# Layer 1's recurrent mixer in another order: four heads' scans at once, a gate pair between the heads' matrices, its convolution and its squares in PSUM

## The chip, the cores and the metric

The kernel runs on one core of a Trainium2 chip. The metric is the device time of one execution in microseconds (us), as the median of several runs. The engines are called PE (TensorE: matmuls, and PEld for its weight loads), DVE (VectorE), ACT (ScalarE), POOL (GpSimd) and SP (SyncE, which issues the loads here).

## What is computed

One sequence of 256 tokens of width 1024 goes through two residual layers and then a second block. Layer 0 has a convolution and an attention mixer, layer 1 the recurrent mixer `mixer_c`; each is followed by a squared-ReLU MLP of width 4096. The change touches layer 1's mixer and the end of each MLP.

```python
def rg_lru(x, w_r, b_r, w_i, b_i, lam):
    """x: (B, S, W). h_t = a_t h_{t-1} + sqrt(1-a_t^2) (i_t x_t)."""
    b, s, w = x.shape
    xb = x.reshape(b, s, LRU_HEADS, LRU_BLOCK)          # 8 heads of 128
    r = jax.nn.sigmoid(jnp.einsum("bshi,hij->bshj", xb, w_r) + b_r).reshape(b, s, w)
    i = jax.nn.sigmoid(jnp.einsum("bshi,hij->bshj", xb, w_i) + b_i).reshape(b, s, w)
    log_a = -LRU_C * r.astype(jnp.float32) * jax.nn.softplus(-lam.astype(jnp.float32))
    a = jnp.exp(log_a)
    mult = jnp.sqrt(-jnp.expm1(2.0 * log_a))
    bx = mult * (i * x).astype(jnp.float32)
    ...
    _, hseq = lax.associative_scan(combine, (a, bx), axis=1)
    return hseq.astype(x.dtype)

def mixer_c(h, w_in, conv_w, conv_b, w_r, b_r, w_i, b_i, lam, w_out):
    u = h @ w_in
    gate, xr = jnp.split(u, 2, axis=-1)
    xr = causal_depthwise_conv(xr, conv_w) + conv_b     # width 4
    y = rg_lru(xr, w_r, b_r, w_i, b_i, lam) * jax.nn.gelu(gate)
    return y @ w_out

def sq_relu_mlp(h, w_up, w_down):
    return jnp.square(jax.nn.relu(h @ w_up)) @ w_down

for layer in range(DEPTH):
    h = rmsnorm(x, mix_norm[layer])
    ...
    x = x + y
    x = x + sq_relu_mlp(rmsnorm(x, mlp_norm[layer]), w_up[layer], w_down[layer])
```

## The kernel before

Activations lie transposed: a tile of 128 partitions holds 128 channels, and its 256 columns are the tokens; `[128, 8, 256]` is the whole width. Each product of fp32 matrices is made of three matmuls (`mm3`): every operand is split into a high part that the matmul takes exactly and a low part, the rest, and high by high, low by high and high by low are added in PSUM. So each weight block of 128 by 1024 (a "unit", 512 KB, loaded by SP in the order of `weight_plan`) is copied to `wh` by ACT or DVE and subtracted to `wl` by DVE or POOL. POLICY says which: the first letter is the engine of `wh`, the second that of `wl` (g for POOL). A unit of a square projection is 24 matmuls with 256 columns. Four buffers hold raw units, and six hold split ones. `wh`, `wl` of a unit are made when the unit two places ahead of it is used.

PSUM is two rings of four banks, `mm` and `acc`. A bank holds a pair of `[128, 256]` outputs. A new tile of a ring takes the bank of the tile four before it, and waits until the last reader of that is done.

A tile framework puts the instructions of each engine into one fixed order, by the order of the code and by its own estimate of times, and adds the semaphores. At run time each engine takes its instructions strictly in that order.

Layer 1's mixer (`layer1`, L953 on):

- `gfirst` makes the first two pairs of `xr`, the input projection of the recurrent branch; two more pairs follow. R, the norm's factor by token, is spread to all partitions between the second and the third pair (L426, L432) and multiplied in as DVE reads a pair from PSUM (L998).
- The convolution: ACT writes the last tap with the bias to an `acc` bank `ca` (L1002), and DVE adds three taps (L1006); the third goes to `xc` in SBUF.
- `ri(u)` does four heads, 0 to 3 or 4 to 7: ACT copies a head's `xc` to `xch` and DVE subtracts `xcl` (`split`, L383 and L391); PE makes the two gates of the head, r and i, in an `acc` bank (6 matmuls); ACT takes two tanh (L982, L983), and DVE makes (ig+1)·xc (L984). Then for each head th = tanh(..) and r = exp(..) (L986, L987), and for each pair of heads DVE squares r into `xc` (L990) and makes (r²+1)·th (L991).
- After all eight heads: two square roots on ACT (L1021), then the four gate pairs `cg` (`gate_pair`: PE, a DVE multiply L1012, a Gelu on ACT L1014), ig·th (L1025), a scan for each head on DVE (L1028), the product with the gate (L1030) and the split into `xr` (again used, as the high part) and `ysl`. Then the output projection `wo1`, whose first matmuls need the first pair of heads.

`ri(0)` stands ahead of the last `xr` pair and `ri(1)` behind it.

`proj_tail` ends a projection bank by bank; at the end of an MLP it also squares the new x on ACT into an SBUF tile `sqt` (L826, L824) and DVE adds it to `s` (L828). Layer 1's MLP is followed by `b2_head`, whose first matmuls go to `d["c0"]`, a new `mm` tile.

## Time and profile before

| | |
|---|---|
| median of 3 runs | 854.93 us (853.67 to 857.74) |
| span of the profiled execution | 859.5 us |
| PE busy in it | 817.3 us, 95% |
| DVE busy in it | 612.3 us, 71% |
| ACT, POOL busy in it | 457.5 us, 226.1 us |
| layer 1's mixer | 311 to 418 us of that span |

How to read it: the times of single instructions are all from the one profiled execution, counted in us from its first instruction. The page shows of it only the span. A PE matmul is listed with 0.28 us, but the next starts 0.118 us after it, or 0.213 us after it where the granted clock is half; the distance of starts is its cost. Likewise the instructions of DVE and ACT overlap a little, so their cost in a row is taken from the distance of starts. In a merged row with "x4" the time is that of all four.

### The profile page before, as it was taken

To read this page: it belongs to the slowest core of one execution; us is meant where nothing else is said; L and a number is where in the kernel's file an instruction comes from. 1 tells how busy PE (TensorE), PEld (TensorE's weight loads), DVE (VectorE), ACT (ScalarE), POOL (GpSimd) and SP (SyncE) were. 2 spreads that over 40 slices of the span, in tenths; PEclk is the share of its full clock that TensorE was granted. 3 is DMA by queue.
4 is the path that set the end of the run, shared out by engine and by line. 5 is a ranking of instruction groups with operands and counts; after the bars stand their busy time and mean duration, and the time that the engine had idled before them with its cause. 6 is when DMAs were issued, how large, how long until landed. Compare 5 with 4: busy or idle time off the path is not lost.

```text
span 859.5 us, 16183 instructions
## 1 busy us (share of the span) xinstructions
PE 817.3 (95%) x6472; PEld 783.3 (91%) x6472; DVE 612.3 (71%) x969; ACT 457.5 (53%) x718; POOL 226.1 (26%) x160
## 2 busy tenths in 40 slices
PE   6988999999999999769999999999999999999996
PEld 6976799999999989769999999999988988889996
DVE  5999878999885488997668554447543786655753
ACT  5456556434355444555756444445535577775432
POOL 4784745101111146550314111111100022220001
PEclk9999899999999998898999999999999999999998
DMA  6764247878887543336574655665343532555531
GB/s 227 264 180 145 74 137 270 281 268 288 301 270 244 177 143 124 98 110 211 190 239 158 199 190 181 191 178 165 107 147 115 180 123 75 150 193 162 186 96 49
DMA packets 41258, 152.30 MB, mean 177 GB/s; under 512 B 4576, under 2 KB 5088, under 8 KB 39008
## 3 DMA queue, kind: packets, MB, share of 16 engines
q1 hardware_dynamic: 40752, 149.19, 53.3%
q10 hardware_dynamic: 432, 2.10, 0.7%
q8 instruction: 50, 0.82, 0.4%
q14 instruction: 24, 0.20, 0.1%
HBM read 149.17 MB, written 2.10 MB: 176 GB/s over the span
## 4 chain that ended last, share of the span: by engine, by line
PE 63%; DVE 23%; issue 6%; DMA 3%; ACT 3%; POOL 1%; SPq 0%; DVEq 0%; POOLq 0%; ACTq 0%
PE mm L344 10%; PE mm L345 10%; PE mm L346 10%; PE acc L345 9%; PE acc L346 8%; PE acc L344 8%; DVE wl L299 4%; DVE mm L553 3%; DMA mw<-in_modw 3%; DVE mdump L854 3%; PE acc L1284 2%; PE acc L1312 2%; PE mm L1321 2%; DVE st L638 1%; ACT wh L296 1%
## 5 line engine op out<-in xcount | busy, mean ns | idle before, releaser
L296 ACT ACTIVATE wh<-raw 128x1024 fp32r<-128x1024 f32 (+1 forms) x233 | 243.3, 1050 | 247.5 <-PE mm L345 103.5
L299 DVE TENSOR_TENSOR wl<-raw,wh 128x1024 fp32r<-128x1024 f32 (+1 forms) x201 | 252.1, 1261 | 138.6 <-ACT wh L296 136.6
L346 PE MATMUL mm<-xsh,wl 128*128 128x256 f32 x992 | 280.9, 283 | 2.3 <-DVE wl L299 1.4
L344 PE MATMUL mm<-xsh,wh 128*128 128x256 f32 x992 | 282.6, 285 | 0.0
L345 PE MATMUL mm<-xsl,wh 128*128 128x256 f32 x992 | 280.8, 283 | 1.6 <-DVE xsl L818 1.6
L344 PEld LDWEIGHTS mm<-xsh,wh 128*128 128x128 f32 x992 | 189.8, 191 | 3.7 <-issue 3.3
L346 PEld LDWEIGHTS mm<-xsh,wl 128*128 128x128 f32 x992 | 189.7, 191 | 2.8 <-DVE wl L299 1.6
L345 PEld LDWEIGHTS mm<-xsl,wh 128*128 128x128 f32 x992 | 189.8, 191 | 2.3 <-DVE xsl L818 1.8
L346 PE MATMUL acc<-mah,wl 128*128 128x256 f32 x512 | 143.0, 279 | 1.0 <-DVE wl L299 1.0
L345 PE MATMUL acc<-mal,wh 128*128 128x256 f32 x512 | 143.0, 279 | 0.4 <-DVE mal L391 0.4
L344 PE MATMUL acc<-mah,wh 128*128 128x256 f32 x512 | 143.3, 280 | 0.0
L299 POOL TENSOR_TENSOR wl<-raw,wh 128x1024 fp32r<-128x1024 f32 x42 | 105.5, 2533 | 71.3 <-ACT wh L296 45.5
L928 POOL TENSOR_TENSOR ma<-mr 128x512 f32<-128x512 f32 x32 | 51.3, 1606 | 253.0 <-ACT mr L926 248.3
L346 PEld LDWEIGHTS acc<-mah,wl 128*128 128x128 f32 x512 | 96.2, 188 | 1.4 <-DVE wl L299 1.4
L345 PEld LDWEIGHTS acc<-mal,wh 128*128 128x128 f32 x512 | 96.3, 188 | 0.6 <-DVE mal L391 0.6
L344 PEld LDWEIGHTS acc<-mah,wh 128*128 128x128 f32 x512 | 96.3, 188 | 0.0
L854 DVE CUSTOM_DVE_ANT_0 mdump<-mw,cv 128x1024 f32<-128x1024 f32 x40 | 50.2, 1256 | 3.8 <-DMA mw<-in_modw 3.6
L345 PE MATMUL acc<-ysl,wh 128*128 128x256 f32 x128 | 38.3, 301 | 7.2 <-DVE ysl L391 7.2
L553 DVE SCALAR_TENSOR_TENSOR mm<-z,cwh,mm 128x256 f32<-128x256 f32 x106 | 44.6, 476 | 0.2
L1303 POOL TENSOR_SCALAR P<-P,st 128x512 f32<-128x512 f32 x32 | 22.3, 698 | 84.2 <-DVE st L1302 57.0
L391 DVE TENSOR_TENSOR mal<-ma,mah 128x512 fp32r<-128x512 f32 x32 | 22.8, 714 | 16.8 <-POOL ma L928 16.8
L345 PEld LDWEIGHTS acc<-ysl,wh 128*128 128x128 f32 x128 | 26.2, 205 | 8.0 <-DVE ysl L391 7.6
(346 smaller groups left out, 1364.8 us busy)
## 6 DMA issues: line engine op xcount, KB each, us to landing
raw<-in_wst SPq DMA_DIRECT2D x240, 512.0 KB, 3.7
mw<-in_modw SPq DMA_DIRECT2D x12, 1024.0 KB, 7.2
nb<-in_nab SPq DMA_DIRECT2D x16, 256.0 KB, 3.6
ab<-in_alibi ACTq DMA_DIRECT2D x1, 1536.0 KB, 9.5
x<-in_xT SPq DMA_DIRECT2D x4, 256.0 KB, 4.4
cv<-in_cvec SPq DMA_DIRECT2D x1, 1024.0 KB, 4.8
cx<-in_cT SPq DMA_DIRECT2D x1, 1024.0 KB, 4.8
xd<-x SPq DMA_DIRECT2D x1, 1024.0 KB, 4.5
```

The costliest lines, as they stand in the source:

```text
L296: nc.scalar.activation(wh, r, AF.Copy)
L299: (nc.vector if lo == "v" else nc.gpsimd).tensor_tensor(wl, r, wh.bitcast(F32), op=ALU.subtract)
L344: mm(out, w[0], x[0], start=start, stop=False, skip_group_check=True)
L345: mm(out, w[0], x[1], start=False, stop=False, skip_group_check=True)
L346: return mm(out, w[1], x[0], start=False, stop=stop, skip_group_check=True)
L391: self.nc.vector.tensor_tensor(l, src, h.bitcast(F32), op=ALU.subtract)
L553: return V.scalar_tensor_tensor(conv[:, j] if i == 30 else ca, zs, c, ca, op0=ALU.mult, op1=ALU.add)
L854: V.tensor_tensor_reduce(d, w, cv[:, s * 1024:(s + 1) * 1024], 0.5, 0.0, op0=ALU.mult, op1=ALU.add, accum_out=self.mod[:, s * 24 + i:s * 2 ...
L928: G.tensor_tensor(a, r, r, op=ALU.mult)
L1284: PE.matmul(sc[i], Q[tag, h][a][:, qs], K[tag, h][b], start=a + b == 0, stop=a == 1)
L1303: G.tensor_scalar(P, P, st[:, 3:4], 0.0, op0=ALU.mult, op1=ALU.add)
L1312: PE.transpose(pt[:, i * 128:(i + 1) * 128], P[:, i * 128:(i + 1) * 128], self.ident)
```

## The change

- The convolution's third tap stays in the PSUM bank `ca`; the split, and (ig+1)·xc, read it there. The four banks are all of the `acc` ring, so the heads' gates go to the `mm` ring.
- The square of r is made by ACT into an `acc` bank; DVE reads it from there. DVE's four squares go.
- The square root, ig·th and the four scans of a group of four heads stand in `ri` right behind those heads. Two table loads of ACT come with it, since tanh and exp come once more between the two square roots.
- The first gate pair stands ahead of `ri(1)`, and `weight_plan` is changed to match; the product with the gate and the split follow pair by pair.
- The high part of every second `cg` unit is copied by ACT instead of DVE.
- The squares of x at the end of both MLPs go to `mm` banks.

```diff
-POLICY.update(..., ri=("vg",), cg=("vg",))
+POLICY.update(..., ri=("vg",), cg=("vg", "ag"))
...
-    ri(1)
     for j in range(8):
+        if j == 2:
+            ri(1)
         inn("cg", w, j * 128)
...
             for i, (st, scaled) in enumerate(sums):
-                q = st if b == 0 else self.t(mp, [128, 2, T], f"sqt{i}", bufs=2)
+                q = st if b == 0 else self.pair(self.ps())
...
+        cas = {}
+        sls = [slice(4 * b, 4 * b + 4) for b in range(2)]
         def ri(u):
...
-                self.split(xc[:, h], xch, xcl)
-                ps = self.ps("acc")
+                self.split(ca, xch, xcl)
+                ps = self.ps()
...
-                V.scalar_tensor_tensor(ig[:, h], ig[:, h], 1.0, xc[:, h], op0=ALU.add, op1=ALU.mult)
+                V.scalar_tensor_tensor(ig[:, h], ig[:, h], 1.0, ca, op0=ALU.add, op1=ALU.mult)
...
-                    V.tensor_tensor(xc[:, sl], r[:, sl], r[:, sl], op=ALU.mult)
-                    V.scalar_tensor_tensor(th[:, sl], xc[:, sl], 1.0, th[:, sl], op0=ALU.add, op1=ALU.mult)
-            return last
+                    a2 = self.pair(self.ps("acc"))
+                    last = S.activation(a2, r[:, sl], AF.Square)
+                    V.scalar_tensor_tensor(th[:, sl], a2, 1.0, th[:, sl], op0=ALU.add, op1=ALU.mult)
+            sl = sls[u]
+            with self.tc.issue_after(last.ins):
+                sq = S.activation(th[:, sl], th[:, sl], AF.Sqrt, scale=0.25)
+            V.tensor_tensor(ig[:, sl], ig[:, sl], th[:, sl], op=ALU.mult)
+            for h in hs:
+                V.tensor_tensor_scan(xc[:, h], r[:, h], ig[:, h], 0.0, op0=ALU.mult, op1=ALU.add)
+            return sq
...
-                    V.scalar_tensor_tensor(xc[:, j] if i == 2 else ca[:, h], xr[:, j, i:i + T],
+                    V.scalar_tensor_tensor(ca[:, h], xr[:, j, i:i + T],
...
-        ex = ri(1)
+        gate_pair(0)
+        with self.tc.issue_after(sq.ins):
+            sq = ri(1)
         ys = (self.t(lp, [128, 8, T], "xr", F32R), self.t(lp, [128, 8, T], "ysl", F32R))
-        sls = [slice(4 * b, 4 * b + 4) for b in range(2)]
-        for sl in sls:
-            with self.tc.issue_after(ex.ins):
-                sq = S.activation(th[:, sl], th[:, sl], AF.Sqrt, scale=0.25)
         for p in range(4):
-            gate_pair(p)
...
+            if p:
+                gate_pair(p)
+            hp = slice(2 * p, 2 * p + 2)
             with self.tc.issue_after(sq.ins):
+                S.activation(gl[:, hp], gl[:, hp], AF.Gelu_apprx_tanh)
+            V.tensor_tensor(xc[:, hp], xc[:, hp], gl[:, hp], op=ALU.mult)
+            self.split(xc[:, hp], ys[0][:, hp], ys[1][:, hp])
```

The fixed order of the engines moves with it. In the names of the rows below, `acc_3856`, `acc_3866`, `acc_3937` and `acc_4082` or `acc_4090` are the convolution's banks of the pairs 0 to 3, `xch`, `xcl` a head's high and low part, `r`, `ig`, `th` the gates' tiles.

First, ACT at the heads 0 to 3, before, from the convolution's first base to the first exp:

```order
L1002 ACTIVATE acc_3856<-xr_3714,par_69 128x256 x2
L1002 ACTIVATE acc_3866<-xr_3714,par_69 128x256 x2
L383 ACTIVATE xch_3952<-xc_3716 128x256
L383 ACTIVATE xch_3966<-xc_3716 128x256
L1002 ACTIVATE acc_3937<-xr_3714,par_69 128x256 x2
L982 ACTIVATE r_3717<-acc_3956,hb_1869 128x256
L983 ACTIVATE ig_3719<-acc_3956,hb_1869 128x256
L982 ACTIVATE r_3717<-acc_3970,hb_1869 128x256
L983 ACTIVATE ig_3719<-acc_3970,hb_1869 128x256
L383 ACTIVATE xch_3980<-xc_3716 128x256
L383 ACTIVATE xch_3994<-xc_3716 128x256
```

and after the change, the same place:

```order
L1018 ACTIVATE acc_3866<-xr_3714,par_69 128x256
L297 ACTIVATE wh_4061<-raw_4059 128x1024
L1018 ACTIVATE acc_3866<-xr_3714,par_69 128x256
L384 ACTIVATE xch_3952<-acc_3856 128x256
L1018 ACTIVATE acc_3937<-xr_3714,par_69 128x256 x2
L987 ACTIVATE r_3717<-mm_3956,hb_1869 128x256
L988 ACTIVATE ig_3719<-mm_3956,hb_1869 128x256
L991 ACTIVATE th_3718<-r_3717,sm_1843 128x256
L992 ACTIVATE r_3717<-r_3717,sm_1843 128x256
L384 ACTIVATE xch_3966<-acc_3856 128x256
L384 ACTIVATE xch_3980<-acc_3866 128x256
L987 ACTIVATE r_3717<-mm_3970,hb_1869 128x256
```

The copy of head 1 (`xch_3966`) stood right behind that of head 0, and now stands behind head 0's two gates, its th and its exp. On PE, all 48 matmuls of the last `xr` pair stood ahead of head 0's first or between the matmuls of the heads 0 to 3; now 4 stand there, and the other 44 follow behind head 3.

Second, DVE ahead of the low part of head 4. Before, two rows of the convolution's last pair stood around it:

```order
L1006 SCALAR_TENSOR_TENSOR acc_4082<-xr_3714,par_69,acc_4082 128x256
L991 SCALAR_TENSOR_TENSOR th_3718<-xc_3716,th_3718 128x512
L1006 SCALAR_TENSOR_TENSOR acc_4082<-xr_3714,par_69,acc_4082 128x256
L391 TENSOR_TENSOR xcl_4098<-xc_3716,xch_4097 128x256
L1006 SCALAR_TENSOR_TENSOR acc_4082<-xr_3714,par_69,acc_4082 128x256
```

and after the change (`xcl_4168` is the low part of head 4, L1003 the scans):

```order
L997 SCALAR_TENSOR_TENSOR th_3718<-acc_4019,th_3718 128x512
L1014 TENSOR_TENSOR xr_3714<-mm_4028,R_3850 128x2x256
L1001 TENSOR_TENSOR ig_3719<-ig_3719,th_3718 128x1024
L299 CAST wh_4252<-raw_4250 128x1024
L1003 SCALAR_TENSOR_TENSOR xc_3716<-r_3717,ig_3719 128x256 x4
L1022 SCALAR_TENSOR_TENSOR acc_4090<-xr_3714,par_69,acc_4090 128x256
L392 TENSOR_TENSOR xcl_4168<-acc_3937,xch_4167 128x256
```

The product ig·th, a weight copy and the four scans of the heads 0 to 3 now stand ahead of it.

Third, DVE at the end of layer 1's MLP, after the change (`mm_6864` and `mm_6866` are the squares of the third bank; before, these rows read `sqt` tiles in SBUF):

```order
L300 TENSOR_TENSOR wl_6916<-raw_6913,wh_6915 128x1024
L807 TENSOR_TENSOR mtmp_6893<-acc_4724,R_865_5781 128x512
L829 TENSOR_TENSOR s_4_75<-s_4_75,mm_6864 128x512
L808 TENSOR_TENSOR x_74<-x_74,mtmp_6893 128x512
L829 TENSOR_TENSOR s_5_76<-s_5_76,mm_6866 128x512
```

The ring `mm` is now taken by six squares ahead of `c0`; `c0` is the fourth tile behind `mm_6864`, so its bank is that one.

## Rows read from the trace of the kernel before

**Rows 1.** The page's first line and, of its first part, the lines of PE and DVE: busy us, share of the span, instructions.

```profile
span 859.5 us, 16183 instructions
PE 817.3 (95%) x6472; PEld 783.3 (91%) x6472; DVE 612.3 (71%) x969; ACT 457.5 (53%) x718; POOL 226.1 (26%) x160
```

**Rows 2.** Windows of layer 1's mixer: from and to, then the length and the busy us of PE, PEld, DVE, ACT, POOL with their instructions, then the granted clock of PE, the DMA share and GB/s.

```profile
331.00:343.00 12.00, 11.41 (x89) 10.64 (x89) 11.74 (x20) 5.73 (x15) 7.05 (x4) 1.00 0.43 132
343.00:363.00 20.00, 14.89 (x101) 13.99 (x100) 19.70 (x33) 10.48 (x26) 9.53 (x4) 0.83 0.32 105
363.00:378.00 15.00, 15.00 (x130) 15.00 (x129) 14.96 (x14) 10.00 (x16) 7.93 (x3) 1.00 0.35 106
378.00:392.00 14.00, 5.28 (x25) 4.87 (x24) 14.00 (x16) 8.35 (x11) 5.61 (x2) 0.66 0.27 78
```

**Rows 3.** Timeline of PE in the same stretch, the longest of its waits: start, length, what it does, and in brackets the idle time before it and who ended it.

```profile
345.16 0.38 PE L345 MATMUL acc<-xcl,wh 128*128 128x256 f32 x1 [1.49 <-DVE xcl L391]
...
356.44 0.58 PE L345 MATMUL acc<-xcl,wh 128*128 128x256 f32 x1 [2.07 <-DVE xcl L391]
...
380.83 0.39 PE L344 MATMUL acc<-xr,wh 128*128 128x256 f32 x1 [2.52 <-ACT xr L383]
...
387.43 0.58 PE L345 MATMUL acc<-ysl,wh 128*128 128x256 f32 x1 [6.21 <-DVE ysl L391]
```

**Rows 4.** Timeline of PE: two neighbours at half clock, the first matmul behind the spreading of R, two neighbours at full clock, and the last at half clock behind the wait at 387.43.

```profile
324.01 0.41 PE L345 MATMUL mm<-xsl,wh 128*128 128x256 f32 x1
324.23 0.41 PE L346 MATMUL mm<-xsh,wl 128*128 128x256 f32 x1
...
328.47 0.37 PE L344 MATMUL mm<-xsh,wh 128*128 128x256 f32 x1
...
332.00 0.28 PE L346 MATMUL mm<-xsh,wl 128*128 128x256 f32 x1
332.12 0.28 PE L344 MATMUL mm<-xsh,wh 128*128 128x256 f32 x1
...
392.50 0.40 PE L344 MATMUL acc<-xr,wh 128*128 128x256 f32 x1
```

**Rows 5.** Timeline of DVE in layer 1's mixer.

```profile
331.16 0.49 DVE L1006 SCALAR_TENSOR_TENSOR acc<-xr,par,acc 128x256 f32<-128x256 f32 x1 [0.70 <-ACT acc L1002]
...
334.08 2.44 DVE L1006 SCALAR_TENSOR_TENSOR acc<-xr,par,acc 128x256 f32<-128x256 f32 x6
...
341.23 2.42 DVE L984 SCALAR_TENSOR_TENSOR ig<-ig,xc 128x256 f32<-128x256 f32 x1
...
343.96 0.41 DVE L984 SCALAR_TENSOR_TENSOR ig<-ig,xc 128x256 f32<-128x256 f32 x1
...
348.62 1.89 DVE L298 CAST wh<-raw 128x1024 fp32r<-128x1024 f32 x3
...
351.42 2.46 DVE L991 SCALAR_TENSOR_TENSOR th<-xc,th 128x512 f32<-128x512 f32 x1
...
374.20 2.44 DVE L1025 TENSOR_TENSOR ig<-ig,th 128x1024 f32<-128x1024 f32 x2
...
377.74 1.26 DVE L1028 TENSOR_TENSOR_SCAN xc<-r,ig 128x256 f32<-128x256 f32 x2
...
379.50 5.52 DVE L1028 TENSOR_TENSOR_SCAN xc<-r,ig 128x256 f32<-128x256 f32 x2
```

**Rows 6.** Timeline of POOL in the same stretch.

```profile
349.43 9.16 POOL L299 TENSOR_TENSOR wl<-raw,wh 128x1024 fp32r<-128x1024 f32 x3 [6.06 <-DVE wh L298]
...
378.87 5.61 POOL L299 TENSOR_TENSOR wl<-raw,wh 128x1024 fp32r<-128x1024 f32 x2 [5.86 <-ACT wh L296]
```

**Rows 7.** Timeline of ACT in the same stretch.

```profile
329.90 2.27 ACT L1002 ACTIVATE acc<-xr,par 128x256 f32<-128x256 f32 x4 [0.76 <-DVE xr L998]
336.94 0.81 ACT L383 ACTIVATE xch<-xc 128x256 fp32r<-128x256 f32 x2 [4.77 <-DVE xc L1006]
...
340.35 0.48 ACT L982 ACTIVATE r<-acc,hb 128x256 f32<-128x256 f32 x1 [0.86 <-PE acc L346]
340.73 0.47 ACT L983 ACTIVATE ig<-acc,hb 128x256 f32<-128x256 f32 x1
...
342.41 1.10 ACT L986 ACTIVATE th<-r,sm 128x256 f32<-128x256 f32 x2
343.39 1.09 ACT L987 ACTIVATE r<-r,sm 128x256 f32<-128x256 f32 x2
...
367.69 1.28 ACT L1021 ACT_TABLE_LOAD   x1
368.99 1.07 ACT L1021 ACTIVATE th<-th 128x1024 f32<-128x1024 f32 x1
```

**Rows 8.** Timeline of DVE at the end of layer 0's MLP, the two long ones.

```profile
311.70 2.43 DVE L818 SCALAR_TENSOR_TENSOR xsl<-x,par,xsh 128x256 fp32r<-128x256 f32 x2
...
314.65 2.90 DVE L828 TENSOR_TENSOR s<-s,sqt 128x512 f32<-128x512 f32 x1
```

**Rows 9.** Timeline of PE at the start of layer 1's first pairs: the matmul that waited for the last low part.

```profile
319.13 0.39 PE L345 MATMUL mm<-xsl,wh 128*128 128x256 f32 x1 [1.56 <-DVE xsl L818]
```

**Rows 10.** Timeline of DVE at the end of layer 1's MLP: the sum that reads the third bank's square.

```profile
596.58 0.68 DVE L828 TENSOR_TENSOR s<-s,sqt 128x512 f32<-128x512 f32 x1
```

**Rows 11.** Timeline of PE there: the first matmul of `c0`.

```profile
595.64 0.28 PE L344 MATMUL mm<-hch,wh 128*128 128x256 f32 x1
```

More of the change, by code (lines that the diff above doesn't have):

```diff
@@ L40 @@
 POLICY = {n: ("ag",) for n in ("gate", "val", "q", "k", "v", "wo0")}
-POLICY.update(val=("av", "ag", "av", "ag"), gate=("av", "av", "av", "ag"), xr=("av", "ag"), ri=("vg",), cg=("vg",))
+POLICY.update(val=("av", "ag", "av", "ag"), gate=("av", "av", "av", "ag"), xr=("av", "ag"), ri=("vg",), cg=("vg", "ag"))
 POLICY["wo0"] = ("ag",) * 7 + ("av",)
@@ L974, in ri @@
             for h in hs:
+                ca = cas[h // 2][:, h % 2]
                 xch = self.t(lp, [128, T], "xch", F32R, bufs=2)
                 xcl = self.t(lp, [128, T], "xcl", F32R, bufs=2)
-                self.split(xc[:, h], xch, xcl)
-                ps = self.ps("acc")
+                self.split(ca, xch, xcl)
+                ps = self.ps()
                 for i in range(2):
@@ L989, in ri, with gate_pair @@
                     sl = slice(h - 1, h + 1)
-                    V.tensor_tensor(xc[:, sl], r[:, sl], r[:, sl], op=ALU.mult)
-                    V.scalar_tensor_tensor(th[:, sl], xc[:, sl], 1.0, th[:, sl], op0=ALU.add, op1=ALU.mult)
-            return last
+                    a2 = self.pair(self.ps("acc"))
[8 more added lines that the diff above has]
+            return sq
+        def gate_pair(p):
+            ps = self.gpair(("cg", "cg"), xs)
+            V.tensor_tensor(gl[:, 2 * p:2 * p + 2], self.pair(ps), self.b2(R), op=ALU.mult)
         for p in range(4):
             if 2 * p == RI0:
-                ri(0)
+                sq = ri(0)
             ps = pss[p] if p < 2 else self.gpair(("xr", "xr"), xs)
             V.tensor_tensor(xr[:, 2 * p:2 * p + 2, 3:], self.pair(ps), self.b2(R), op=ALU.mult)
-            ca = self.pair(self.ps("acc"))
+            ca = cas[p] = self.pair(self.ps("acc"))
             for h in range(2):
@@ L1005, in layer1 @@
                     j = 2 * p + h
[L1006 removed]
+                    V.scalar_tensor_tensor(ca[:, h], xr[:, j, i:i + T],
                                            self.p("ccw", j * 4 + i), ca[:, h], op0=ALU.mult, op1=ALU.add)
[L1009 to L1031 removed]
+        gate_pair(0)
+        with self.tc.issue_after(sq.ins):
+            sq = ri(1)
+        ys = (self.t(lp, [128, 8, T], "xr", F32R), self.t(lp, [128, 8, T], "ysl", F32R))
+        for p in range(4):
+            if p:
+                gate_pair(p)
+            hp = slice(2 * p, 2 * p + 2)
+            with self.tc.issue_after(sq.ins):
+                S.activation(gl[:, hp], gl[:, hp], AF.Gelu_apprx_tanh)
+            V.tensor_tensor(xc[:, hp], xc[:, hp], gl[:, hp], op=ALU.mult)
+            self.split(xc[:, hp], ys[0][:, hp], ys[1][:, hp])
         acc = [self.ps("acc") for _ in range(4)]
```

15 lines of the change are left out of this document (removed).

## Prediction

> **What bounds the kernel now.** I read first the page's busy shares: PE is busy 95% of the span [rows 1], so only time in which PE waits, or runs at half clock, can be gained or lost. The windows of layer 1's mixer come next: between 343 and 363 us and between 378 and 392 us PE is busy 14.9 of 20 us and 5.3 of 14 us, the granted clock falls to 0.83 and 0.66, and DVE is busy throughout, 60 of 61 us [rows 2]. The timeline of PE then names who ends its waits: DVE's low parts of the heads (1.49, 2.07 us) and the first pair for the output projection (2.52 and 6.21 us) [rows 3]. So DVE's order sets the pace here. Why DVE is slow stands in its own timeline: (ig+1)·xc takes 0.41 us once and 2.42 us another time, th 2.46 us, two scans 5.52 instead of 1.26 us [rows 5], always while POOL makes a low part of a weight [rows 6]. The convolution's steps, which read one operand in PSUM, take 2.44 us for six even while POOL runs [rows 5].
>
> What PE loses here: a matmul costs 0.118 us at full clock (2.4 GHz) and 0.213 us at half (1.2 GHz) [rows 4]. From 328.47 us [rows 4] to the output projection lie 48 + 48 (the last two xr pairs) + 48 (eight heads) + 192 (gate) = 336 matmuls, 39.6 us; so it could begin at 368.1. It goes on at 387.43 [rows 3] with 3 matmuls done: 19.0 us lost. From there to 392.5 it runs at half clock [rows 4], 24 matmuls with 0.095 us more each, 2.3 us. Together **21.3 us** before.
>
> **The change, part by part.** I lay the new order of the engines end to end with the old durations. These are, by distance of starts: a convolution step 0.39, a low part 0.40, a multiply of 512 columns 0.60, a weight copy on DVE 0.60, ig·th 1.2, a scan 0.59 [rows 5]; on ACT a base of the convolution 0.57, a head's copy 0.40, r and ig 0.37 each, th and exp 0.50 each, a table load 1.28, the root 1.06 [rows 7], and about 1.05 for a weight copy (estimate, from the root of the same 1024 columns).
>
> *A, heads 0 to 3.* PE ends the third xr pair at 328.47 + 48 × 0.118 = 334.1. DVE starts the convolution at 331.16 [rows 5]; four steps bring it to 332.7. The second pair's steps wait for ACT, which has now four bases and a weight copy to make from 329.90 on: 333.2. Five steps, the third pair's multiply, one more step and head 0's low part end at 336.7. Head 0 leaves PE at 337.4. Now ACT makes two bases, r, ig, th, exp and only then the copy of head 1: 339.7. DVE has a weight copy and three steps between, head 1's low part ends at 340.6, heads 1 and 2 leave PE at 342.0. ACT needs seven more (r, ig, th, r, ig, exp, th) until the copy of head 3, 344.8; head 3 leaves PE at 345.9. That is 11.8 us for 24 + 4 matmuls worth 3.3: **8.5 us lost**. Before, the 48 matmuls of the last xr pair filled such waits.
>
> A row bears on this: DVE's first step waited until 331.16 although head 0's own base ended at 330.47; it waited for both bases of the bank [rows 5, 7]. The Trainium skill, page PSUM — Partial Sum Buffer, section "PSUM bank collisions raise a hardware error", says that PSUM must be guarded by bank, because two engines may not touch one bank at the same time even at different places. By that rule ACT's copy of a pair's second head must not start before DVE's last read for the first one, where before the two copies ran back to back from SBUF in 0.81 us [rows 7]. The rule speaks against a convolution that stays in PSUM; without it copies and low parts could stand ahead, and A would lose about 5 us less (the 2.3 us from 337.4 to 339.7 and the 2.8 us from 342.0 to 344.8), and the sum would be near 855.
>
> *B, the scans ahead of head 4.* Behind head 3 PE has 44 + 48 matmuls, until 356.8. ACT makes r, ig, th, exp, the square (0.60), a table load, the root: 350.8, then a weight copy to 351.9; the table load lies under PE's 92 matmuls. POOL takes that weight until 354.3 and holds up ig·th, which ends at 355.5; the copy on DVE ends at 356.1 and starts POOL again; so do ACT's copy at 355.0 and a second POOL turn. Two scans run into two POOL turns, as at 379.50 [rows 5, 6]: the scans end at 362.9 and head 4's low part, which stands behind them on DVE, at 363.7. PE waits **6.8 us**. If POOL is never in the way it is 0 (all ends near 356.9); I take 6.8, because the row at 379.50 is the same meeting of the same two instructions.
>
> *C, heads 4 to 7.* The same chain as A, with 28 matmuls: head 4 leaves PE at 364.3; DVE has five convolution steps, a weight copy and a gate multiply ahead of head 4's (ig+1)·xc (367.3), and ACT's copies of the heads 5 and 6 follow it (368.1); heads 5 and 6 leave at 369.3; r, ig, r, ig, th, th and the copy of head 7 take until 371.7, and head 7 leaves at 372.9. 9.2 us for 3.3 us of matmuls: **5.9 us lost**. The second table load (back to tanh) lies under B's wait; if B is 0, it costs up to 1.28.
>
> *D, the output projection.* Behind head 7 PE has 140 matmuls, 16.5 us, until 389.4. Root, Gelu, four scans and the first pair end by 386 to 389 even if POOL steps in twice. So the old waits of 2.52 and 6.21 us and their half clock go: **0 lost**. This is the gain of the change.
>
> *Clock.* Behind the wait of 6.21 us the clock stood at half, and that cost 2.3 us (above). A and C are two such stretches, 4.6 us, and of the matmuls in their chains about 20 lie one behind the other, 20 × 0.095 = 1.9 us. What A loses so (2.4 us) comes off B's wait, whose end DVE and POOL set. Net **4.1 us**.
>
> Layer 1: 8.5 + 6.8 + 5.9 + 0 + 4.1 = 25.3 against 21.3: **+4.0 us**. DVE itself gets lighter: four squares of 0.60 and four weight copies of 0.60 go to ACT; the moved reads from PSUM cost about 0.06 us more each. They stand in the chains above.
>
> *The end of layer 0's MLP.* The sum at 314.65 took 2.90 us [rows 8]; from PSUM it need not. But the new order puts the low parts of the third bank ahead of the fourth bank's multiply, and they meet POOL as one did before (2.43 us [rows 8]). By the same laying end to end the last low part comes at 318.65 instead of 319.1 [rows 9]: **−0.45 us**.
>
> *The end of layer 1's MLP.* `c0` takes the bank of the third bank's square, and its first matmul must now wait for the sum that reads it. That sum ends about 597.2 [rows 10]; `c0` began at 595.64 [rows 11]. PE has nothing else in its order: **+1.6 us**, between 0 and 4.4 (with half clock behind it as behind 319.13 [rows 9]: from 321.9 to 327.9, estimate 2.8).
>
> Sum: +4.0 − 0.45 + 1.6 = +5.15. The profiled execution spans 859.5 us [rows 1], 4.6 above the median of 854.93; the sum is 864.65 against the span, and as a difference 860.1 against the median.
>
> **Rivals.** *Two short meetings.* POOL's turns miss the scans (B near 0), the rest as above: layer 1 loses 8.5 + 0 to 1 + 5.9 + 4.1 = 19, 2.3 less than before, and with +1.15 outside it 853.8. For it: which of two starts first is decided within 0.1 us in my walk; against: the scans have POOL's turns of 2.8 us [rows 6] on both sides. It decides where the scans end before 356.9.
>
> *Faster.* The waits on POOL go with the operands. In rows: (ig+1)·xc 2.0, th 1.8, scans 4.3 us too long [rows 5]; if the heads' chains then keep the clock at full, layer 1 loses 8.5 + 0 + 5.9 = 14.4 instead of 21.3, and the time is 854.93 − 6.9 + 1.15 = 849.2. The Trainium skill, page SBUF — State Buffer, section "Who interferes with whom", says that a VectorE instruction with at most one SBUF input does not contend with GpSimd. By that rule the trace agrees for the convolution's steps [rows 5]; but the scans keep two SBUF inputs.
>
> *More.* The clock stays at half through both chains and falls once more behind `c0`: 3 us + 2.8 us on top, 866.
>
> *Evens out.* A is shorter than walked, since ACT's rows overlap better, by some 3 us: 857.
>
> **How the numbers follow.** Forecast 0.40, more 0.10, evens out 0.12, two short meetings 0.22, faster 0.16. About 0.5%, 4.3 us, is what a measurement of this kernel can tell from no change: faster lies below 850.7, slower above 859.2. So slower 0.50, same 0.34, faster 0.16. The range reaches from 851 to 867: it leaves out most of the faster case and little above.
>
> **What would show it.** Right: PE's waits in the profile of the changed kernel for copies of the heads 1, 3, 5, 7 by ACT (2 us each) and for one low part of DVE behind the scans (5 to 7 us); no wait over 1 us at the output projection; a wait of 1.6 us of `c0` for DVE. Wrong: head 4's low part without a wait; scans of 0.6 us each beside POOL; the clock at 1.00 from 340 to 375; a wait of PE for the first pair of the output projection, as before.

## The result and the profile after

The changed kernel takes 862.10 us (median of 4 runs, 861.26 to 862.76) against 854.69 us (4 runs) of the kernel before: ratio 1.0071, 95% interval 1.0047 to 1.0095. A second set (after_again, below) gave 1.0083 (1.0053 to 1.0113). It is slower; forecast was 860.1, a ratio of 1.006.

The page of after, its first line and the line of PE to POOL:

```profile
span 860.7 us, 16173 instructions
...
PE 817.5 (95%) x6472; PEld 782.6 (91%) x6472; DVE 593.7 (69%) x961; ACT 465.7 (54%) x728; POOL 222.2 (26%) x160
```

DVE has 18.6 us less to do than in [rows 1], and PE's busy time is the same. The spans differ by only 1.2 us, the times by 7.4: the profiled execution of before was a long one (its second profile, below, spans 854.4 us). So I compare stretches, not totals.

The windows of layer 1's mixer in after, columns as in [rows 2]:

```profile
331.00:343.00 12.00, 7.10 (x31) 6.39 (x32) 7.67 (x18) 7.85 (x20) 2.37 (x1) 0.56 0.27 86
343.00:363.00 20.00, 13.54 (x96) 13.05 (x95) 14.75 (x19) 10.42 (x16) 11.49 (x5) 0.84 0.35 106
363.00:378.00 15.00, 11.63 (x69) 11.34 (x70) 4.68 (x11) 11.32 (x22) 4.72 (x3) 0.65 0.17 42
378.00:392.00 14.00, 14.00 (x120) 14.00 (x119) 13.62 (x16) 10.25 (x13) 3.46 (x2) 1.00 0.50 150
```

The poor windows have moved. Before, they were the second and the last; now they are the first (7.1 of 12 us, clock 0.56) and the third (0.65), while DVE is idle a third of the time or more. The last window is full. In the poor windows DVE is no longer what sets the pace. The timeline of PE in after says what does:

```profile
323.18 0.36 PE L345 MATMUL mm<-xsh,wh 128*128 128x256 f32 x1
...
329.97 0.39 PE L345 MATMUL mm<-xch,wh 128*128 128x256 f32 x1 [0.91 <-ACT xch L384]
331.25 0.38 PE L346 MATMUL mm<-xcl,wh 128*128 128x256 f32 x1 [0.90 <-DVE xcl L392]
...
334.42 0.86 PE L345 MATMUL mm<-xch,wh 128*128 128x256 f32 x2 [2.32 <-ACT xch L384]
...
340.03 0.58 PE L345 MATMUL mm<-xch,wh 128*128 128x256 f32 x1 [2.33 <-ACT xch L384]
...
342.12 0.41 PE L347 MATMUL mm<-xch,wl 128*128 128x256 f32 x1
...
360.03 0.58 PE L346 MATMUL mm<-xcl,wh 128*128 128x256 f32 x1 [4.92 <-DVE xcl L392]
...
364.19 0.85 PE L345 MATMUL mm<-xch,wh 128*128 128x256 f32 x2 [2.73 <-ACT xch L384]
...
369.36 0.58 PE L345 MATMUL mm<-xch,wh 128*128 128x256 f32 x1 [2.18 <-ACT xch L384]
...
371.45 0.41 PE L347 MATMUL mm<-xch,wl 128*128 128x256 f32 x1
...
389.06 0.28 PE L345 MATMUL acc<-xr,wh 128*128 128x256 f32 x1
```

The first row is the first matmul behind the spreading of R, the last one the first of the output projection, which does not wait. Between them lie 389.06 − 323.18 = 65.9 us for the same 39.6 us of matmuls: **26.3 us lost**, where before lost 21.3. Four waits of 2.2 to 2.7 us are for ACT's copies of the heads 1, 3, 5 and 7, and one of 4.92 us is for DVE's low part of head 4. The rows at 342.12 and 371.45 are the last matmuls of the heads 3 and 7. DVE and POOL at that low part, and DVE's second group of scans:

```profile
352.59 6.68 DVE L1003 TENSOR_TENSOR_SCAN xc<-r,ig 128x256 f32<-128x256 f32 x4
...
359.56 0.41 DVE L392 TENSOR_TENSOR xcl<-acc,xch 128x256 fp32r<-128x256 f32 x1
...
380.16 2.44 DVE L1003 TENSOR_TENSOR_SCAN xc<-r,ig 128x256 f32<-128x256 f32 x4
```

```profile
352.81 5.33 POOL L300 TENSOR_TENSOR wl<-raw,wh 128x1024 fp32r<-128x1024 f32 x2 [1.82 <-PE mm L347]
```

Four scans of one shape take 6.68 us beside POOL's two turns and 2.44 us without POOL.

The two ends of an MLP in after: PE's wait for the last low part at the end of layer 0's (answering to [rows 9]), and `c0` at the end of layer 1's (answering to [rows 11]); then DVE's sum, which `c0` waits for (answering to [rows 10]):

```profile
315.91 0.38 PE L346 MATMUL mm<-xsl,wh 128*128 128x256 f32 x1 [0.60 <-DVE xsl L819]
...
596.75 0.39 PE L345 MATMUL mm<-hch,wh 128*128 128x256 f32 x1 [1.51 <-DVE s L829]
```

```profile
596.02 0.67 DVE L829 TENSOR_TENSOR s<-s,mm 128x512 f32<-128x512 f32 x1
```

### The profile page after: what moved, and what is told of

Its sections match the earlier page's. It is cut to its first block, busy times and chain, and to the rows that moved or that the text cites. A ratio compares the mean times of both kernels' runs of the same rounds, so it can differ in the third digit from the quotient of the medians.

```text
span 860.7 us, 16173 instructions
## 1 busy us (share of the span) xinstructions
PE 817.5 (95%) x6472; PEld 782.6 (91%) x6472; DVE 593.7 (69%) x961; ACT 465.7 (54%) x728; POOL 222.2 (26%) x160
## 4 chain that ended last, share of the span: by engine, by line
PE 67%; DVE 19%; issue 5%; ACT 4%; DMA 4%; POOL 1%; SPq 0%; DVEq 0%; POOLq 0%; ACTq 0%
PE mm L345 12%; PE mm L346 12%; PE mm L347 12%; PE acc L346 8%; PE acc L347 8%; PE acc L345 8%; DVE wl L300 4%; DVE mm L554 3%; DMA mw<-in_modw 3%; DVE mdump L855 2%; PE acc L1288 2%; PE acc L1316 2%; PE mm L1325 2%; ACT wh L297 1%; DVE st L639 1%
## 5 line engine op out<-in xcount | busy, mean ns | idle before, releaser
L297 ACT ACTIVATE wh<-raw 128x1024 fp32r<-128x1024 f32 (+1 forms) x237 | 247.5, 1050 | 240.8 <-PE mm L346 91.9
L300 POOL TENSOR_TENSOR wl<-raw,wh 128x1024 fp32r<-128x1024 f32 x42 | 102.0, 2449 | 75.3 <-ACT wh L297 50.6
L346 PE MATMUL acc<-ysl,wh 128*128 128x256 f32 x128 | 36.9, 290 | 1.0 <-DVE ysl L392 1.0
```

The costliest lines, as they stand in the source:

```text
L297: nc.scalar.activation(wh, r, AF.Copy)
L300: (nc.vector if lo == "v" else nc.gpsimd).tensor_tensor(wl, r, wh.bitcast(F32), op=ALU.subtract)
L346: mm(out, w[0], x[1], start=False, stop=False, skip_group_check=True)
```

## The experiments

"PE lost" is worked out as in the prediction: from the first matmul behind the spreading of R to the first of the output projection, less 39.6 us; where the output projection waits again, that wait and the half clock behind it (0.095 us a matmul) are added. It is of the one profiled execution, whose own time stands in the column before it: for tail_sbuf, cg_sq and psum_ops that was the fastest one, 2.9 to 3.9 us below the median, for early_pair 2.3 us above it. Each ratio is to runs of the kernel before on the same chip.

| kernel | median us | before beside it | ratio (95% interval) | profiled, us | PE lost us |
|---|---|---|---|---|---|
| before_again | 856.34 | 856.59 | 0.9999 (0.9978 to 1.0020) | 856.32 | 20.7 |
| after | 862.10 | 854.69 | 1.0071 (1.0047 to 1.0095) | 862.76 | 26.3 |
| after_again | 863.82 | 855.70 | 1.0083 (1.0053 to 1.0113) | 864.55 | 27.6 |
| tail_sbuf | 862.10 | 856.59 | 1.0056 (1.0038 to 1.0074) | 858.18 | 24.3 |
| scans_late | 860.13 | 857.36 | 1.0043 (1.0024 to 1.0061) | 859.66 | 24.7 |
| b_nopool | 858.54 | 855.70 | 1.0032 (1.0015 to 1.0049) | 859.04 | 22.3 |
| fill | 860.43 | 857.36 | 1.0028 (1.0007 to 1.0048) | 860.41 | 23.3 |
| conv_sbuf | 855.31 | 856.59 | 0.9984 (0.9967 to 1.0000) | 855.47 | 20.4 |
| conv_sbuf_acc | 853.81 | 856.59 | 0.9963 (0.9945 to 0.9980) | 852.81 | 17.9 |
| cg_sq | 852.73 | 857.36 | 0.9938 (0.9915 to 0.9962) | 849.83 | 16.1 |
| psum_ops | 850.67 | 855.70 | 0.9933 (0.9909 to 0.9957) | 847.16 | 14.3 |
| early_pair | 850.35 | 857.36 | 0.9925 (0.9900 to 0.9949) | 852.60 | 14.8 |

The time follows the last column: from 27.6 to 14.3 us lost, 13.3 us, the ratio falls by 0.015, 12.8 us.

**Both kernels once more** (no edit).

> The kernel before once more, unchanged, for a second profile. Its first profile spans 859.5 us while the median time is 854.7; the profile of after spans 860.7 at a time of 862.8. So the two spans differ by 1.2 us and the times by 7.4. Theory: the first profile of before had losses that most executions do not have; 28 matmuls at half clock behind the wait at 319.13 (2.8 us) are the candidate, and some 2.7 us ahead of 300 us. A second profile then spans about 853, with full clock between 321 and 328 us, and layer 1 loses about 21 us on PE as in the first. Rival: the half clock is always there, and the difference of times comes from layer 1; then the second profile shows the half clock again, and layer 1 loses less than 21 us, some 17.

> The changed kernel once more, beside the other kernels of this call on one chip. Theory: 0.5 to 0.7% above the kernel before, as the steps of the prediction (+5.15 us) and its first measurement (1.0071) say; its profile shows layer 1 losing about 26 us on PE again, with the same waits (2.3, 2.3, 4.9, 2.7, 2.2 us). Rival: the first profile was an unlucky execution, and layer 1 loses 21 to 23; then the difference is below 0.4%.

Layer 1 lost 20.7 us again in before (first profile 21.3) and 27.6 in after (26.3), so these losses belong to the kernels and not to one execution. The second profile of before spans 854.4 us, forecast about 853. Of the half clock behind the last low part, 28 matmuls in the first profile, 15 came again, here seen in the window and the first of these matmuls:

```profile
316.00:324.00 8.00, 7.77 (x54) 7.56 (x53) 5.75 (x6) 2.39 (x3) 5.09 (x5) 0.79 0.53 186
```

```profile
315.37 0.39 PE L345 MATMUL mm<-xsl,wh 128*128 128x256 f32 x1 [1.51 <-DVE xsl L818]
...
317.93 0.42 PE L345 MATMUL mm<-xsl,wh 128*128 128x256 f32 x1
```

From layer 1's first matmul to the first behind the spreading of R lie the same 104 matmuls in all profiles. The starts in before (the other one is at 328.47 [rows 4]), in its second profile, and in after (the other one is at 323.18, above):

```profile
310.75 0.28 PE L344 MATMUL mm<-xsh,wh 128*128 128x256 f32 x1
```

```profile
307.00 0.28 PE L344 MATMUL mm<-xsh,wh 128*128 128x256 f32 x1
...
323.17 0.36 PE L344 MATMUL mm<-xsh,wh 128*128 128x256 f32 x1
```

```profile
308.09 0.28 PE L345 MATMUL mm<-xsh,wh 128*128 128x256 f32 x1
```

The stretch takes 17.7 and 16.2 us in before, 15.1 in both profiles of after. So the change gains 2.6 or 1.1 us here: the wait is shorter, and no half clock follows it. Of the 5.1 us between the two spans of before 1.6 lie in this stretch and 3.7 ahead of it. Layer 1's first matmul starts anywhere from 305.8 to 310.8 us in the 13 profiles, without regard to the kernel.

**The tails' squares back in SBUF.**

```diff
-                q = st if b == 0 else self.pair(self.ps())
+                q = st if b == 0 else self.t(mp, [128, 2, T], f"sqt{i}", bufs=2)
```

> After the change, with the squares at the ends of the MLPs back in SBUF tiles (that part undone). Theory: the wait of c0 for DVE's sum (1.51 us in after) goes, and the end of layer 0's MLP loses what it gained: 0.45 by the prediction's walk, 0.96 by the waits at the last low part (1.56 before, 0.60 after). So 862.1 - 1.5 + 0.5 to 1.0, about 861.3, within 1 us of after. Rival one: the squares in PSUM cost more than the wait shows, and the result comes down by 3 us or more, to 859 or below. Rival two: they also kept the clock up behind the first pairs; without them the half clock of 2.8 us comes back, 864.

`c0`'s wait is gone from PE's waits, and the wait for the last low part is 1.51 us again, with full clock behind it this time (granted clock 1.00 from 315 to 321 us):

```profile
315.00 0.39 PE L346 MATMUL mm<-xsl,wh 128*128 128x256 f32 x1 [1.51 <-DVE xsl L819]
...
317.28 0.36 PE L345 MATMUL mm<-xsh,wh 128*128 128x256 f32 x1
```

The waits differ by −1.51 and +0.91 us. By the distance of starts the two effects are −1.7 us (output projection to `c0`, 206.0 us for 207.7 in after) and +0.6 us (layer 1's first matmul to the third pair, 15.65 us for 15.09). The ratio is lower than after's two (1.0056 to 1.0071 and 1.0083), as it should be by so little, but the intervals overlap: its size is not settled by times. No half clock came in this profile, against rival two. Rival one, 3 us less than after, is a ratio of 1.0036 or 1.0048, by after's two sets; the times do not exclude the second, but the stretches leave no room for 3 us. In layer 1 the instructions stand exactly as in after, and yet it lost 24.3 us for 26.3 and 27.6: it has 42 single matmuls at half clock there, after 70 and 74. So one profile's loss is good to 2 or 3 us, and small differences of it prove nothing.

**The convolution's result back in SBUF**, first with the gates left in `mm`, then with the gates in `acc` too.

```diff
-                ca = cas[h // 2][:, h % 2]
+                ca = xc[:, h]
...
-                    V.scalar_tensor_tensor(ca[:, h], xr[:, j, i:i + T],
+                    V.scalar_tensor_tensor(xc[:, j] if i == 2 else ca[:, h], xr[:, j, i:i + T],
```

> After the change, with the convolution's third tap written to xc in SBUF again, and the split and (ig+1) xc reading it there; the heads' gates stay in the mm ring. ACT's order then has the copies of heads 0 and 1 side by side, and those of heads 2 and 3 nearly. Theory of the bank (a copy of a pair's second head may not start before DVE's last read for the first one): the waits of 2.3 us for copies of heads 1 and 3 and of 2.7 and 2.2 us for heads 5 and 7 go, and each half clock behind them in part: about -5 to -8, 854 to 857. Theory of the ring: the heads' gates take the four mm banks, so the matmuls of the last xr pair, which need a bank of the same ring, still stand behind the heads; a PE wait of 1 to 2 us stays at each pair of heads, now for gates' or copies' ends, -2 to -3: 859 to 860. Rival: DVE's reads from SBUF meet POOL again (2.4 instead of 0.4 us each), and the wait of head 4's low part grows: 862 or more.

The result lies where the theory of the bank put it: the loss is 20.4 us, and the ratio fell by 0.009 to 0.010, 7.4 to 8.5 us. ACT makes the first two copies back to back again. On PE the waits for copies of the later heads are short (the row at 336.69 is the last matmul of head 3), and there is one of 9.16 us behind the scans:

```profile
327.50 0.81 ACT L384 ACTIVATE xch<-xc 128x256 fp32r<-128x256 f32 x2 [1.03 <-DVE xc L1022]
```

```profile
331.72 0.39 PE L345 MATMUL mm<-xch,wh 128*128 128x256 f32 x1 [0.51 <-ACT xch L384]
332.75 0.58 PE L345 MATMUL mm<-xch,wh 128*128 128x256 f32 x1 [0.65 <-ACT xch L384]
...
336.69 0.28 PE L347 MATMUL mm<-xch,wl 128*128 128x256 f32 x1
...
356.33 0.58 PE L346 MATMUL mm<-xcl,wh 128*128 128x256 f32 x1 [9.16 <-DVE xcl L392]
```

```profile
347.96 6.62 DVE L1003 TENSOR_TENSOR_SCAN xc<-r,ig 128x256 f32<-128x256 f32 x4
```

PE is through with head 3 4.3 us sooner (14.9 us behind that first matmul, for 19.2), but the scans still meet POOL (6.62 us), and half of what A gave turns into a longer wait in B: the low part of head 4 reaches PE 34.4 us behind the spreading of R (first matmul at 321.95), in after 36.9. The rest of the gain, 3.4 us, is in C. Then, in addition:

```diff
-                ps = self.ps()
+                ps = self.ps("acc")
```

> As conv_sbuf, and the heads' gates in the acc ring again, as before the change; the rest of the change stays (squares of r by ACT into PSUM, scans by four heads, gate pair ahead of heads 4 to 7, second cg copies by ACT, tails in PSUM). In its order on PE the matmuls of the last xr pair and of a gate pair stand between the heads' again. Theory of the ring: most of A and C (8.5 and 5.9 us lost in the prediction; waits of 0.9, 0.9, 2.3, 2.3 and 2.7, 2.2 us and about 9 us of half clock in after) goes; what stays is the wait behind the scans (up to 5 us) and c0: 848 to 853, below the kernel before. Theory of the bank alone: no more than conv_sbuf gives. Rival: DVE's order sets the pace, as in before; then the waits come back as waits for DVE's low parts and the time is that of before, 855 to 857.

With this the matmuls of the last `xr` pair and of a gate pair stand between the heads' in PE's order again, since they need no bank that the heads' gates hold. The loss is another 2.5 us less, and the longest wait at a head is 2.57 us. The time is just outside the forecast of the ring theory (853.8 for 848 to 853), since a wait now comes last that the theories had not named there: the output projection's for its first pair, whose product stands on DVE behind the second scans.

```profile
377.00 1.22 PE L345 MATMUL acc<-xr,wh 128*128 128x256 f32 x4 [6.60 <-ACT xr L384]
```

**Step B: the scans ahead of head 4.** One kernel moves the first group's product and scans behind the heads 4 to 7 in the code; the other takes POOL out of their way.

```diff
-            V.tensor_tensor(ig[:, sl], ig[:, sl], th[:, sl], op=ALU.mult)
-            for h in hs:
-                V.tensor_tensor_scan(xc[:, h], r[:, h], ig[:, h], 0.0, op0=ALU.mult, op1=ALU.add)
...
             sq = ri(1)
+        scans(0)
+        scans(1)
```

> After the change, but ig th and the four scans of the heads 0 to 3 written behind the heads 4 to 7 (the square root stays where it is). In DVE's order head 4's low part then stands ahead of all four scans. Theory of the prediction's step B: PE's wait of 4.92 us for that low part goes but for half a us, A and C stay as they are (waits for copies of 2.3, 2.3, 2.7 and 2.2 us), the output projection waits for at most 1 us: about 5 us less than after, 0.1% above the kernel before (857). Rival one: the meeting of scans and POOL only moves; the scans then stand between the low parts of the heads 4 to 7 and lengthen C by what B loses: 860 to 862. Rival two: B's wait was set by ACT's chain up to the square root and ig th, not by the scans: a wait of 3 us or more stays for head 4.

```diff
-cg=("vg", "ag"))
+cg=("vg", "ag", "vv", "av", "vg", "ag", "vg", "ag"))
```

> After the change, with the low parts of two cg units (the third and fourth) made by DVE instead of POOL, so that POOL makes nothing while the first four scans run. DVE gets two subtractions of 1.2 us more (its row of that kind in the run conv_sbuf_acc), and in its order both stand ahead of the scans. Theory of step B (the meeting of the scans and POOL): the four scans take 2.4 us as the second four did, instead of 6.7; with one subtraction of 1.2 between them and the weight's release, PE's wait for head 4's low part falls from 4.9 to about 2 us: 2.5 to 3 us less than after. Rival: the scans stay slow without POOL (they wait for something else, the square root or PSUM), and the wait stays at 4.9 or grows by the 1.2 to 2.4 us of the subtractions: as after, or 1 to 2 us more.

In scans_late the low part of head 4 came in time and the wait moved, rival one: PE waits 8.11 us, for the copy of head 5. ACT's row says why:

```profile
361.82 0.86 PE L345 MATMUL mm<-xch,wh 128*128 128x256 f32 x2 [8.11 <-ACT xch L384]
```

```profile
354.73 2.39 DVE L1006 TENSOR_TENSOR_SCAN xc<-r,ig 128x256 f32<-128x256 f32 x1
...
360.95 0.41 DVE L989 SCALAR_TENSOR_TENSOR ig<-ig,acc 128x256 f32<-128x256 f32 x1
```

```profile
361.39 0.66 ACT L384 ACTIVATE xch<-acc 128x256 fp32r<-128x256 f32 x2 [6.31 <-DVE ig L989]
```

ACT stood idle 6.31 us, released by DVE's (ig+1)·xc at 360.95. That instruction reads head 4's half of the bank, the copy head 5's half. Both only read: nothing but the bank ties them; and DVE's read stood behind the scans, two of them of 2.4 us beside POOL (one is shown), and behind steps of the convolution's last pair, a gate multiply and a weight copy. The loss, 24.7 us, is no less than that of tail_sbuf. Without POOL the scans are short, and the low part comes in time:

```profile
351.14 2.43 DVE L1003 TENSOR_TENSOR_SCAN xc<-r,ig 128x256 f32<-128x256 f32 x4
...
353.86 0.42 DVE L392 TENSOR_TENSOR xcl<-acc,xch 128x256 fp32r<-128x256 f32 x1
```

```profile
354.34 0.39 PE L346 MATMUL mm<-xcl,wh 128*128 128x256 f32 x1 [0.30 <-DVE xcl L392]
...
359.50 0.98 PE L345 MATMUL mm<-xch,wh 128*128 128x256 f32 x2 [4.30 <-ACT xch L384]
```

B's wait fell from 4.92 to 0.30 us, more than the 2.5 to 3 that I gave; the copy behind it now waits 4.30 instead of 2.73 us. DVE makes one weight copy more there ahead of the (ig+1)·xc that the copy waits for, and beside POOL it took 1.74 us (at 356.57). The ratio is 0.005 below that of after on the same chip, 4.4 us. The scans' slowness is the meeting with POOL.

**The clock.** Matmuls without use, in banks that are overwritten.

```diff
+                for i in range((6, 14, 0, 14, 30, 16, 0, 12)[h]):
+                    nc.tensor.matmul(ps[:, :T], w[0][:, :128], xs[0][:, i % 8], start=True, stop=True)
```

> After the change, with matmuls added that do no useful work: ahead of the matmuls of the heads 0, 1, 3, 4, 5 and 7 PE makes 6, 14, 14, 30, 16 and 12 products of 256 columns in the bank which that head's gates then overwrite. They lie in PE's waits (0.9 and 0.9, 2.3, 2.3, 4.9, 2.7, 2.2 us; 14 are worth 1.65 us at full clock), so that PE is not idle there. Theory of the prediction's term clock: the matmuls of A and C then run at full clock; after shows 70 or more of them at half, 6.7 us, of which those ahead of B's wait are given back there: 4 to 5 us less than after, 0.1% above the kernel before (857). Rival one: the chain through ACT and DVE sets the pace of the heads, and the clock of the few matmuls in it matters little: 1 us or less, 861. Rival two: the added matmuls delay the heads' real ones, since they take their time ahead of them: 863 or more.

```profile
331.00:343.00 12.00, 9.68 (x68) 9.39 (x67) 7.76 (x19) 7.83 (x18) 2.39 (x1) 0.86 0.31 100
363.00:378.00 15.00, 15.00 (x112) 14.83 (x111) 5.34 (x12) 12.51 (x25) 5.43 (x3) 0.86 0.15 40
```

The granted clock is 0.86 in both windows where after had 0.56 and 0.65. The ratio is 0.003 to 0.0055 below the three kernels of after's order (1.0056 to 1.0083), 2.4 to 4.7 us, although 92 matmuls were added (the table counts them as lost). The test is not a clean one: two waits stayed, 2.32 us for the copy of head 1 and 5.01 us for the low part of head 4, with half clock behind both, and the order changed a little (18 matmuls of the last `xr` pair now stand ahead of head 3, for 4). The size is that of the term, and rival two does not fit. Rival one, at most 1 us, is not excluded: the interval touches that of after and overlaps that of tail_sbuf.

**What of the change helps.** Two parts alone in the old order:

```diff
-cg=("vg",))
+cg=("vg", "ag"))
...
-                    V.tensor_tensor(xc[:, sl], r[:, sl], r[:, sl], op=ALU.mult)
+                    last = S.activation(xc[:, sl], r[:, sl], AF.Square)
```

> The kernel before with only two of the change's parts, both of which take work from DVE: r is squared by ACT (into xc in SBUF, four times 512 columns), and every second cg unit's high part is copied by ACT. No convolution in PSUM, heads and scans in the old order. Theory: DVE's order sets the waits of before (1.5, 2.1, 1.1, 1.7, 6.2 us in its second profile), and 4 to 5 us less on it shorten the waits at the output projection by 2 to 4 us and take their half clock away: 0.3 to 0.5% faster than before, 852 to 854. Rival: what keeps DVE is the meetings with POOL, which stay; no change, 856. Second rival: ACT's squares stand ahead of copies that PE waits for: 857 or more.

This is 0.6% faster than before, by what DVE no longer does; which of the two parts gives it was not separated. The gain is not where the theory put it: the output projection waits 3.65 and 5.18 us, in sum as long as before (2.52 and 6.21). It is ahead of that: up to the output projection PE loses 8.2 us, before 12.8. What DVE still loses beside POOL stands in its timeline:

```profile
354.01 4.25 DVE L984 SCALAR_TENSOR_TENSOR ig<-ig,xc 128x256 f32<-128x256 f32 x2 [0.85 <-ACT ig L983]
358.19 2.89 DVE L991 SCALAR_TENSOR_TENSOR th<-xc,th 128x512 f32<-128x512 f32 x1
```

So the next version gives these two an operand in PSUM where ACT writes anyway, and leaves the convolution in SBUF:

```diff
+                    a2 = self.pair(self.ps("acc"))
+                    last = S.activation(a2, r[:, sl], AF.Square)
+                    V.scalar_tensor_tensor(th[:, sl], a2, 1.0, th[:, sl], op0=ALU.add, op1=ALU.mult)
...
+                S.activation(ps[:, T:], ps[:, T:], AF.Tanh, bias=hb[:, 8 + h:9 + h], scale=0.5)
+                V.scalar_tensor_tensor(ig[:, h], ps[:, T:], 1.0, xc[:, h], op0=ALU.add, op1=ALU.mult)
```

> The kernel before (old order, convolution's result in SBUF, gates in acc banks) with what takes an SBUF operand from DVE without touching the rings' order: ACT squares r into an acc bank, ACT leaves the tanh of ig in the gate's own bank and DVE reads it there for (ig+1) xc; and every second cg unit's high part by ACT. In the run cg_sq (852.7) DVE still lost time where both operands are in SBUF: 4.25 us for two (ig+1) xc, 2.89 and 2.28 us for two th, and the output projection waited 3.65 and 5.18 us. Theory: with one operand in PSUM these take 0.4 and 0.7 us each, as in after, and the output projection comes up to 5 us sooner: 847 to 850, the fastest so far. Rival one: the ring acc is too short for squares and gates together, heads wait for banks on PE, and nothing is won over cg_sq: 852 to 854. Rival two: POOL's turns then meet the scans instead: 851.

```profile
333.60 2.35 DVE L391 TENSOR_TENSOR xcl<-xc,xch 128x256 fp32r<-128x256 f32 x1
...
347.00 0.42 DVE L984 SCALAR_TENSOR_TENSOR ig<-acc,xc 128x256 f32<-128x256 f32 x1
...
352.53 3.02 DVE L391 TENSOR_TENSOR xcl<-xc,xch 128x256 fp32r<-128x256 f32 x2 [1.22 <-ACT xch L383]
...
356.67 0.41 DVE L984 SCALAR_TENSOR_TENSOR ig<-acc,xc 128x256 f32<-128x256 f32 x1
```

```profile
333.31 2.37 POOL L299 TENSOR_TENSOR wl<-raw,wh 128x1024 fp32r<-128x1024 f32 x1 [1.80 <-PE acc L345]
345.21 14.93 POOL L299 TENSOR_TENSOR wl<-raw,wh 128x1024 fp32r<-128x1024 f32 x6 [9.53 <-ACT wh L296]
```

POOL worked from 345.21 on for 14.93 us. In that time (ig+1)·xc took 0.41 to 0.42 us, while two low parts, both operands in SBUF, took 3.02 us. The Trainium skill, page SBUF — State Buffer, section "Who interferes with whom", says that a VectorE instruction with two SBUF inputs contends with a GpSimd one that reads SBUF, and one with at most one such input, outside the 2-port modes, does not; the trace agrees for these. (The prediction quoted the rule without the exception.) One instruction with a single SBUF input was slow beside POOL here, DVE's weight copy: 2.08 us at 348.44, and 0.69 at 344.29 without POOL. PE lost 1.8 us less than in cg_sq, the median is 0.7 us above the forecast's upper edge, and the times of the two cannot be told apart. Rival two gave this time (851), but not by this cause: the scans took 0.7 us each, without a meeting.

**A version to beat both**, on conv_sbuf_acc with the tails in SBUF: the first pair's Gelu, product and split ahead of heads 4 to 7.

```diff
+        sq = gelu(0, sq)
         with self.tc.issue_after(sq.ins):
             sq = ri(1)
...
+        prod(0)
+        for p in range(1, 4):
+            gate_pair(p)
+            gelu(p, sq)
+            prod(p)
```

> A version that should beat both: the kernel of the run conv_sbuf_acc with the tails' squares back in SBUF, and the Gelu, the product and the split of the first pair of heads made right behind the first square root, ahead of the heads 4 to 7 (one more table load on ACT, in its idle time of 4 us there). The output projection's first 48 matmuls (5.7 us) then do not wait for the second group's root and scans. In conv_sbuf_acc the output projection waited 6.6 us for ACT's copy of that pair, with 15 matmuls at half clock behind (1.4 us); c0 waited 1.5 us. Theory: 853.8 - 6.6 - 1.4 - 1.5 + 0.9 (the wait at the end of layer 0's MLP comes back) = 845 to 847. Rival one: the second pair is no earlier than before, since its product stands behind the second scans on DVE; the wait only moves there, less the 5.7 us of cover, and about 1 to 2 us stay: 847 to 849. Rival two: ACT's copy of head 4 stands behind the Gelu, which needs the first gate pair; heads 4 to 7 come later by what is gained: 851 to 853.

850.35 us beside 857.36, slower than the forecast of 845 to 847 but faster than both kernels. The output projection waits no more for its first pair. The gate pairs now wait for weights that POOL and DVE split late, the longest time here, a wait that I had not listed:

```profile
367.05 0.48 PE L345 MATMUL mm<-xsh,wh 128*128 128x256 f32 x2 [2.64 <-DVE wh L299]
```

## Why the prediction was right

**The sum.** Its terms, as measured in after's first profile:

| term | predicted | measured | from |
|---|---|---|---|
| A and B, half clock of A inside | 8.5 + 6.8 | 10.2 + 6.7 | third pair's end 323.18 + 48 × 0.118 = 328.8; head 3's end 342.3, less 28 matmuls; to 360.0, less 93 matmuls |
| C with its half clock | 5.9 + 4.1 | 9.2 | 360.0 to 371.7, less 27 matmuls, 8.4; and 0.8 behind it |
| D | 0 | 0 | no wait at 389.06 |
| layer 1 | 25.3 | 26.3 | |
| less before's | 21.3 | 21.3, then 20.7 | |
| end of layer 0's MLP | −0.45 | −2.6, then −1.1 | 17.7, then 16.2, less 15.1; of it the waits 0.96 (1.56 and 0.60) |
| `c0` | +1.6 | +1.5 | wait 1.51 |
| sum | +5.15 | +3.9; with the second profiles +7.3 | 5.0 or 6.9, −2.6 or −1.1, +1.5 |

The ratio's interval, 4.0 to 8.1 us, holds the forecast's 5.15 and the second sum; the first lies just below it. The mechanism of each step stood: the copies of heads 1, 3, 5 and 7 on ACT, the low part behind the scans (its wait 4.92 us, in the second profile 5.59, by the steps 6.8 − 2.4 = 4.4), a free output projection, the wait of `c0`. A with B was 1.6 us too small, C 0.8 too large. The end of layer 0's MLP was sized at less than half: the prediction used the half clock behind that wait as an estimate for `c0` (2.8 us), but did not count that it could go here. That the sum came so close is in part luck, since these errors cancel in part.

**A and the bank.** The step said that copies could stand ahead without the rule of the bank, and gave about 5 us in A and a time near 855. conv_sbuf took away the sharing of banks: A's loss fell from 10.2 to 5.1 us (from 321.95 + 48 × 0.118 = 327.6 to 336.8, less 35 matmuls), and the time is 855.3. That the time fits as well is luck: only 2.5 of the 5.1 us are left at head 4, and 3.4 us come from C, which the step had not counted. That the wait is one between the two halves of a bank is shown by ACT's 6.31 us in scans_late. It is a wait that the framework's semaphores make. The Trainium skill, page PSUM — Partial Sum Buffer, section "PSUM bank collisions raise a hardware error", says why they must: even reads of one bank by two engines at once collide. What would happen without the wait no run here shows, and a convolution that stays in PSUM with each head in a bank of its own was not tried.

**What the prediction took as given.** That the last pair's matmuls stand behind the heads was read from the order and not priced on its own. It comes from the ring: four convolution banks fill `acc`, the gates move to `mm`, and the pair needs a bank there. conv_sbuf_acc against conv_sbuf puts it at 2.5 us of loss in one profile of each and 0.2% of the time (the intervals overlap), while the output projection lost 8 us more, so the heads' share is larger.

**B.** The rival of two short meetings needed POOL out of the way, and put that 6.3 us below the forecast. It did not happen by itself; b_nopool made it happen, and the wait went, but the time fell by 4.4 us, since the next copy then waited 1.6 us longer.

**The clock.** Before A's share was taken off, the term was 4.6 + 1.9 = 6.5 us; after's first profile has 70 single matmuls at half clock, 70 × 0.095 = 6.7. Net it was 4.1, and fill gave 2.4 to 4.7 back. The half clock behind `c0`, on which the rival "more" built, did not come: full clock right behind the wait (the first matmuls 0.23 and 0.12 us apart, 596.75, 596.98, 597.10).

**The faster rival** was half right: operands in PSUM do end the meetings of the instructions that have them. But no run shows that this alone saves time. cg_sq, with no more operands in PSUM than before, is faster by 0.6%, psum_ops, with them, by 0.7%, and the two cannot be told apart. What made the change slower is the one part, convolution in PSUM with the gates pushed to `mm`: without it (conv_sbuf_acc) the rest of the change is 0.4% faster than before, with it 0.7 to 0.8% slower.

## What to carry to other kernels

Before an intermediate moves to PSUM, list who reads each bank: if two engines take turns at the two halves of one bank, their work is laid in series, and whatever the ring then pushes to other banks can no longer fill the waits. An operand that one engine writes and one other reads, once, in a bank that is there anyway, has none of this cost and frees DVE from POOL (0.41 us beside it, for up to 2.6), though psum_ops shows no clear gain in time by it over cg_sq. And a moved chain is priced by laying all engines' orders end to end, the clock included; one profiled execution can be several us off its median, so compare stretches, with a second profile where a term is small.
